# Branch C's projection beside the last head of branch A, its result kept in DRAM

## The chip, the cores and the metric

The kernel runs on one core of one Trainium2 chip. The metric is the device time of one execution in microseconds, from runs of the kernel before on the chip: 1801.05, 1803.37 and 1803.6, median 1803.37. Lower is better.

Five engines run their own instruction streams and wait for each other by semaphores: TensorE (PE in the profile, its weight loads PEld), VectorE (DVE), ScalarE (ACT), GpSimd (POOL) and SyncE (SP), which here only issues DMAs. POOL, too, issues DMAs.

## The reference, cut to what matters

The function is a small encoder trunk over one sequence of 512 positions, model width 1024, two layers, float32:

```
for l in range(DEPTH):
    xn = rms_norm(x, ln1[l])
    z = xn @ w_in[l]
    a_q, a_i, a_ff, a_fb, a_g, b_u, b_v, c_q, c_k, c_v, gz = jnp.split(z, offsets, axis=-1)
    o_a = hgrn2_bidirectional(a_q, a_i, a_ff, a_fb, lower[l])
    y_a = rms_norm(o_a, a_norm[l]) * silu(a_g)
    y_b = spatial_gating(gelu(b_u), gelu(b_v), w_s[l], b_s[l])
    y_c = window_attention(qh, kh, vh, sink[l])
    gates = sigmoid(gz)
    merged = gates[0] * (y_a @ w_br[l, 0]) + gates[1] * (y_b @ w_br[l, 1]) + gates[2] * (y_c @ w_br[l, 2])
    x = x + merged @ w_out[l]
    hn = rms_norm(x, ln2[l])
    x = x + square(relu(hn @ w_up[l])) @ w_down[l]
return rms_norm(x, final_norm)
```

Branch A is a gated linear recurrence in both directions with four heads, branch B a gated mixing of blocks of positions, branch C a windowed attention. What the change touches is the three products with w_br, their gates and their sum, and the order of the first loads and last stores.

## The kernel before, in words

**Products.** Each float32 product is made of three matmuls of a rounded part and a remainder (high by high, high by low, low by high), lines L193 to L195, L233 to L235 and, for the form of seven products out of eight, L396 to L398. A weight chunk of 128x1024 (512 KB) is loaded by SP into one of two buffers wr, cast by ACT to its high part wh (L188), and DVE subtracts that for the low part wl (L189); wh and wl have two buffers each. Chunks of the seven-product form (wq) are loaded into ten buffers of their own. An accumulator is 128x512 in PSUM; there are four kinds (m, a, c, s) of two.

**Stages.** A layer has a stage for the input projections, where the gates of branches A and C (tanh values, thd) are written to DRAM; a stage of the branches; a stage in which the branch outputs are projected, gated, added and multiplied by w_out (y, mT, wo); and the two feed-forward products (up, dA to dC). Memory in SBUF is given out by stage: buffers of one stage lie where those of the last one lay, and their first writer waits for the last users of that memory.

**The stage of the branches.** `a_head` (L517) computes a head of branch A: seven blocks of scores (at), each out of two exponentials on ACT and products and sums on DVE; then twice a transpose (kT), its copy, a state (stp, st); then the sum av, its norm by way of POOL (rs, L253), the scaled ao, its transpose oT and the head's output on. Each step waits for the one before on another engine. `c_scores` and `c_out` are branch C. `merge_b` (L827) is one of eight parts of B: a gate projection (gz, 24 matmuls), a product yB (12 matmuls), and the gated product mg, which POOL stores to DRAM (mgd, L837). `gate_a` (L841) projects A's output gate (ag, 24 matmuls), four times.

**What sets the order.** A scheduler of the framework puts the instructions of a stage in a fixed order per engine when the program is built. It takes those of the smallest number first that can run; `hp()` puts a statement ahead of the others, and `later(n)` adds n to the number, so that merge_b and gate_a (30000) fill the places where a head or branch C (15000) waits. They are emitted by `fill(0)` behind head 1, `fill(1, 2)` behind head 2, and `fill(3, 4, 5, 6, 7)` behind head 3.

**The stage after.** `gated` (L980) takes A's output and then C's: four gates th are loaded by POOL (L986), 48 matmuls y of `proj_tok` fill four accumulators, DVE multiplies by the gates (L994 for A, L996 for C) and adds C's to A's (L997); this twice for the two halves of the columns (fl). In C's turn PE transposes the sums (mT, L1002), DVE adds B's part (mB, loaded from mgd, L1005), and ACT and DVE split the result into the operands mgh and mgl of wo.

**The start and the end.** The first loads stand in one block with `hp()` (L632 to L653), the first weight chunk in two halves (L642). At the end `done` (L1061) sums squares of the finished rows, and `finish` (L1048) scales rows 0 and 1 or 2 and 3 of the four row tiles and stores them, all stores from SP (L1059).

## Time and profile before

| | us |
|---|---|
| runs | 1801.05, 1803.37, 1803.6 |
| profiled execution, its own time | 1803.97 |
| its span, first to last instruction | 1802.2 |
| PE busy in the span | 1713.4 |
| DVE busy | 1300.1 |
| ACT busy | 1014.7 |
| POOL busy | 128.6 |

The mean granted clock of TensorE over the span is 0.986 of full speed. A row of the timeline gives the start and length in microseconds, the engine, the line, the operation, output and inputs by their names in the program, the tile's size and the number of instructions in the row; in brackets stands how long the engine had been idle, and what it then waited for. A row of the waits gives the total, the number and the longest of the waits of one line for another. A row of the windows gives for a stretch of time the busy time of PE, PEld, DVE, ACT and POOL with their instructions, then the granted clock as a share of full speed, the DMA share and GB/s. The ends of PE's rows are modelled, its starts are measured.

### The profile page before, as it was taken

What the parts mean: (1) busy time and instruction counts of PE and PEld (TensorE: products, weight loads), DVE (VectorE), ACT (ScalarE), POOL (GpSimd) and SP (SyncE); (2) the same over time, 40 slices, a digit from 0 to 9 for tenths busy, and PEclk for the clock granted to TensorE, in tenths of its full rate; (3) what the DMA queues carried; (4) which work ended last, traced back from release to release, by engine and by line L of the source; (5) the groups of instructions that cost most, each with busy time, mean ns of one, the idle gap of its engine ahead of it and who ended that gap; (6) DMA issues with size and microseconds to landing.
All of it is one profiled execution on the core that took longest, in us unless ns stands there. A gap on an engine that the chain in (4) does not pass through costs nothing.

```text
span 1802.2 us, 21912 instructions
## 1 busy us (share of the span) xinstructions
PE 1713.4 (95%) x8024; PEld 1411.0 (78%) x8024; DVE 1300.1 (72%) x2005; ACT 1014.7 (56%) x1704; POOL 128.6 (7%) x177
## 2 busy tenths in 40 slices
PE   5999998999899999999999999899988999999997
PEld 4778877888687888888877887787877878888786
DVE  6886987677465757677889769767674666586867
ACT  5555578666324645454665565878862345545454
POOL 1011210000210000000010112000003000000000
PEclk9999999999899999999999999999999999999999
DMA  7232221222444242332332422121225352332321
GB/s 287 94 134 84 86 71 43 81 83 76 163 153 175 71 139 81 119 100 99 129 117 79 144 91 73 65 71 65 66 75 202 125 187 95 105 105 94 99 77 47
DMA packets 55994, 191.44 MB, mean 106 GB/s; under 512 B 7376, under 2 KB 7888, under 8 KB 55888
## 3 DMA queue, kind: packets, MB, share of 16 engines
q1 hardware_dynamic: 45648, 156.49, 25.9%
q0 software_dynamic: 10240, 33.56, 5.1%
q8 instruction: 63, 1.03, 0.2%
q14 instruction: 43, 0.35, 0.1%
HBM read 173.25 MB, written 16.78 MB: 105 GB/s over the span
## 4 chain that ended last, share of the span: by engine, by line
PE 51%; DVE 6%; ACT 5%; issue 5%; DMA 1%; SPq 0%; POOL 0%; DVEq 0%; POOLq 0%; ACTq 0%
PE up L195 6%; PE up L193 6%; PE up L194 6%; PE dA L396 3%; PE dA L397 3%; PE dA L398 3%; PE dC L396 2%; PE dC L397 2%; PE dC L398 2%; DVE wl L189 2%; ACT wh L188 1%; PE y L233 1%; PE at L524 1%; PE y L234 1%; PE y L235 1%
## 5 line engine op out<-in xcount | busy, mean ns | idle before, releaser
L189 DVE TENSOR_TENSOR wl<-wr,wh 128x1024 fp32r<-128x1024 f32 x171 | 209.6, 1225 | 182.5 <-ACT wh L188 181.8
L188 ACT CAST wh<-wr 128x1024 fp32r<-128x1024 f32 x171 | 179.3, 1049 | 264.5 <-PE up L194 97.7
L188 ACT CAST wh<-wq 128x1024 fp32r<-128x1024 f32 x196 | 206.2, 1052 | 216.4 <-PE dA L397 48.7
L189 DVE TENSOR_TENSOR wl<-wq,wh 128x1024 fp32r<-128x1024 f32 x196 | 238.9, 1221 | 106.9 <-ACT wh L188 102.9
L193 PE MATMUL up<-xh,wh 128*128 128x512 f32 x512 | 199.4, 391 | 3.8 <-ACT wh L188 1.9
L194 PE MATMUL up<-xl,wh 128*128 128x512 f32 x512 | 200.0, 391 | 0.3 <-DVE xl L245 0.2
L195 PE MATMUL up<-xh,wl 128*128 128x512 f32 x512 | 199.1, 390 | 0.8 <-DVE wl L189 0.7
L193 PEld LDWEIGHTS up<-xh,wh 128*128 128x128 f32 x512 | 96.1, 188 | 26.7 <-ACT wh L188 4.5
L195 PEld LDWEIGHTS up<-xh,wl 128*128 128x128 f32 x512 | 96.1, 188 | 22.1 <-DVE wl L189 2.5
L194 PEld LDWEIGHTS up<-xl,wh 128*128 128x128 f32 x512 | 96.1, 188 | 21.2 <-DVE xl L245 1.8
L396 PE MATMUL dA<-wh,sh 128*128 128x512 f32 x256 | 100.8, 394 | 0.5
L397 PE MATMUL dA<-wh,sh 128*128 128x512 f32 x256 | 99.8, 390 | 0.0
L398 PE MATMUL dA<-wl,sh 128*128 128x512 f32 x256 | 89.6, 391 | 0.0
L566 DVE TENSOR_TENSOR ex<-ex 128x512 f32<-128x512 f32 x112 | 75.8, 694 | 4.0 <-ACT kt L541 3.4
L524 PEld LDWEIGHTS at<-qt,kt 128*128 128x128 f32 x448 | 57.7, 192 | 12.5 <-ACT kt L541 6.6
L524 PE MATMUL at<-qt,kt 128*128 128x128 f32 x448 | 59.9, 277 | 6.8 <-DVE qt L539 5.9
L538 ACT ACTIVATE qt<-ex 128x512 f32<-128x512 f32 x56 | 37.7, 674 | 49.3 <-DVE ex L566 45.1
L253 POOL TENSOR_TENSOR rs<-ms,mhalf_t 128x4 f32<-128x4 f32 (+1 forms) x14 | 18.0, 1287 | 606.1 <-DVE ms L251 585.2
L396 PEld LDWEIGHTS dA<-wh,sh 128*128 128x128 f32 x256 | 48.0, 188 | 14.2 <-ACT wh L188 4.3
L398 PEld LDWEIGHTS dA<-wl,sh 128*128 128x128 f32 x256 | 47.9, 188 | 10.3 <-DVE wl L189 0.2
L397 PEld LDWEIGHTS dA<-wh,sh 128*128 128x128 f32 x256 | 48.1, 188 | 9.8
L193 PE MATMUL gz<-xh,wh 128*128 128x512 f32 x128 | 51.4, 401 | 3.9 <-ACT wh L188 3.8
(387 smaller groups left out, 4396.3 us busy)
## 6 DMA issues: line engine op xcount, KB each, us to landing
wr<-in_ws_dram SPq DMA_DIRECT2D x171, 512.0 KB, 3.3
wq<-in_ws_dram SPq DMA_DIRECT2D x112, 512.0 KB, 4.1
thd<-zt POOLq DMA_DIRECT2D x32, 256.0 KB, 2.7
th<-thd POOLq DMA_DIRECT2D x32, 256.0 KB, 4.3
mgd<-mg POOLq DMA_DIRECT2D x16, 256.0 KB, 2.3
mB<-mgd POOLq DMA_DIRECT2D x16, 256.0 KB, 3.3
x<-in_xT_dram SPq DMA_DIRECT2D x8, 256.0 KB, 6.1
xt<-in_xt_dram SPq DMA_DIRECT2D x8, 256.0 KB, 5.2
```

The lines of the kernel that those rows point to most:

```text
L188: nc.scalar.copy(hi, raw)
L189: nc.vector.tensor_tensor(lo, raw, hi.bitcast(F32), ALU.subtract)
L193: nc.tensor.matmul(pt, whi, xhi, start=first, stop=False)
L194: nc.tensor.matmul(pt, whi, xlo, start=False, stop=False)
L195: nc.tensor.matmul(pt, wlo, xhi, start=False, stop=last)
L233: nc.tensor.matmul(pts[t], xh, hi[:, c], start=k == 0, stop=False)
L396: nc.tensor.matmul(pt, xh[:, t], hi[:, c], start=start and k == 0, stop=False, skip_group_check=True)
L397: nc.tensor.matmul(pt, xl[:, t], hi[:, c], start=False, stop=False, skip_group_check=True)
L398: nc.tensor.matmul(pt, xh[:, t], lo[:, c], start=False, stop=k == 3, skip_group_check=True)
L524: nc.tensor.matmul(pt[:, c], kk(st), qq[:, c], start=True, stop=True)
L538: nc.scalar.activation(qt.rearrange(shp, b=nb, h=2), e_q, AF.Exp)
L566: nc.vector.tensor_tensor(o_ap, o_ap, ap_of(ex, i_, [[istep, 2]] + z), ALU.add)
```

## The change

Four edits. First, C's projection (now yC) is emitted in the stage of the branches, under `later(30000)` behind the four `gate_a`. Its four gate tiles per half are loaded into buffers of that stage (tag ch, ten of them, which branch C's queries and keys also use), multiplied in place, and stored by POOL to a new DRAM tensor mcd: eight loads and eight stores of 256 KB more in this stage per layer, while the next stage loads mcd back (mC, eight loads) and has only A's projection (yA). The gates for C are read from DRAM as before. Second, `fill` is called with 0, 1, 2 behind head 1, with 3, 4 behind head 2, and with 5, 6, 7 behind head 3. Third, the first loads and splits stand in blocks with `hp()` of their own. Fourth, the last scalings: rows 0 and 1 of the second half stay one operation of DVE; all others are multiplied by the final norm's weights on DVE earlier (in `done`) and then scaled on ACT; the stores leave from POOL (rows 2 and 3), SP and ACT.

```diff
@@ -630,27 +630,31 @@
 
     def x_load(k):
         t = T("l", "x")
-        nc.sync.dma_start(t, xT[:, k])
+        with hp():
+            nc.sync.dma_start(t, xT[:, k])
         x0.append(t)
 
+    x_load(0)
+
+    raw, hi, lo = sb.tile([P, CW], F32, tag="wr", bufs=WR, name=nm("wr")), *whl()
+    for i in range(2):
+        c = slice(i * S, (i + 1) * S)
+        with hp():
+            nc.sync.dma_start(raw[:, c], ws[CHUNK[(0, "bu", 0)], :, c])
+        with hp():
+            split(raw[:, c], hi[:, c], lo[:, c])
+    ready[(0, "bu", 0)] = hi, lo
+    x_load(1)
+    for i in (1, 2, 3):
+        x_load(2 * i)
+        x_load(2 * i + 1)
+        ready[(0, "bu", i)] = wload(0, "bu", i)
+    for i in range(8):
+        t = T("tv", "xt")
+        with hp():
+            nc.sync.dma_start(t, xt[:, i // 2, (i % 2) * S:(i % 2 + 1) * S])
+        x0r.append(t)
     with hp():
...
         id_t = const(ident, [P, P], name="id_t")
     n1 = norm_feat(0, x0, x0r)
     norm_rows(n1)
...
@@ -933,6 +938,15 @@
             for h, r in enumerate((lo64, hi64)):
                 nc.scalar.copy(yc[j][r, n * P:(n + 1) * P], po[r, h * P:(h + 1) * P])
 
+        def gates(tag, i, fl):
+
+            res = []
+            for t in range(4):
+                z = T(tag, "th")
+                nc.gpsimd.dma_start(z, thd[:, i * 4 + t, fl * S:(fl + 1) * S])
+                res.append(z)
+            return res
+
         def fill(*ds):
             with later(30000):
                 for d in ds:
@@ -959,59 +973,56 @@
         c_run(1)
         c_run(2)
         c_run(3)
-        fill(0)
+        fill(0,1,2)
         with later(15000):
             c_out(*prev)
         head(2)
-        fill(1, 2)
+        fill(3,4)
         head(3)
-        fill(3, 4, 5, 6, 7)
+        fill(5,6,7)
         with later(30000):
             for h in range(4):
                 gate_a()
+
+            ys = y_split(yc, "yh")
+            for fl in range(2):
+                th = gates("ch", 0, fl)
+                pts = proj_tok(ys, "yC", (l, "y", 2, fl), 0)
+                for t in range(4):
+                    with hp():
+                        nc.vector.scalar_tensor_tensor(th[t], th[t], 1.0, pts[t], ALU.add, ALU.mult)
+                    nc.gpsimd.dma_start(mcd[:, fl * 4 + t], th[t])
         end("br")
         begin("Y2")
-        mg = [[None, None] for _ in range(4)]
         ms = [None] * KT
-        grp = 0
-
-        def gated(bi, br, ys):
-            nonlocal grp
-            for fl in range(2):
-                th = []
-                for t in range(4):
-                    z = T("th", "th")
-                    nc.gpsimd.dma_start(z, thd[:, (1 - bi) * 4 + t, fl * S:(fl + 1) * S])
-                    th.append(z)
-                pts = proj_tok(ys, f"y{br}", (l, "y", br, fl), grp)
-                grp ^= 1
-                for t in range(4):
-                    with hp():
-                        if bi == 0:
-                            mg[t][fl] = T("mg", "mg")
-                            nc.vector.scalar_tensor_tensor(mg[t][fl], th[t], 1.0, pts[t], ALU.add, ALU.mult)
-                        else:
-                            nc.vector.scalar_tensor_tensor(th[t], th[t], 1.0, pts[t], ALU.add, ALU.mult)
-                            nc.vector.tensor_tensor(mg[t][fl], mg[t][fl], th[t], ALU.add)
...
         for h in range(4):
             nc.vector.scalar_tensor_tensor(oa[h], oa[h], 0.5, sg[h], ALU.mult, ALU.mult)
-        gated(0, 0, y_split(oa, "yi"))
-        gated(1, 2, y_split(yc, "yh"))
+        ys = y_split(oa, "yi")
+        for fl in range(2):
+            th = gates("th", 1, fl)
+            mc = []
+            for t in range(4):
+                m = T("mg", "mC")
+                nc.gpsimd.dma_start(m, mcd[:, fl * 4 + t])
+                mc.append(m)
+            pts = proj_tok(ys, "yA", (l, "y", 0, fl), 1 - fl)
+            for t in range(4):
+                with hp():
+                    nc.vector.scalar_tensor_tensor(th[t], th[t], 1.0, pts[t], ALU.add, ALU.mult)
+                    nc.vector.tensor_tensor(mc[t], mc[t], th[t], ALU.add)
+            for d in range(4 * fl, 4 * fl + 4):
+                pt = PT("c" if fl else "s", "mT")
+                for t in range(4):
+                    nc.tensor.transpose(pt[:, t * P:(t + 1) * P], mc[t][:, (d % 4) * P:(d % 4 + 1) * P], id_t)
+                hi, lo = T("yi", "mgh", F32R), T("yi", "mgl", F32R)
+                m = T("th", "mB")
+                nc.gpsimd.dma_start(m, mgd[:, d])
+                with hp():
+                    nc.vector.tensor_tensor(m, m, pt, ALU.add)
+                    split(m, hi, lo)
+                ms[d] = (hi, lo)
         xr = [[T("l", "xr"), T("l", "xr")] for _ in range(4)]
@@ -1020,8 +1031,7 @@
                 nc.gpsimd.dma_start(xr[t][fl], xsrc[:, t, fl * S:(fl + 1) * S])
         n2 = norm_tok("ln2", l, xr, False)
         for fl in range(2):
-            pts = proj_tok(ms, "wo", (l, "wo", fl), grp)
-            grp ^= 1
+            pts = proj_tok(ms, "wo", (l, "wo", fl), 1 - fl)
             for t in range(4):
                 with hp():
                     nc.vector.scalar_tensor_tensor(xr[t][fl], pts[t], 0.5, xr[t][fl], ALU.mult, ALU.add)
@@ -1052,11 +1062,12 @@
             rc = rstd_c(ss, D)
             for fl in range(2):
                 for i, t in enumerate(ts):
-                    if fl == 0 and ts[0] == 0:
+                    if (t // 2, fl) == (0, 1):
+                        nc.vector.scalar_tensor_tensor(xr[t][fl], xr[t][fl], rc[:, i:i + 1], fn_t[fl], ALU.mult, ALU.mult)
+                    else:
                         nc.scalar.activation(xr[t][fl], xr[t][fl], AF.Copy, scale=rc[:, i:i + 1])
-                    else:
-                        nc.vector.scalar_tensor_tensor(xr[t][fl], xr[t][fl], rc[:, i:i + 1], fn_t[fl], ALU.mult, ALU.mult)
-                    nc.sync.dma_start(out[:, t, fl * S:(fl + 1) * S], xr[t][fl])
+                    q = nc.gpsimd if t > 1 else nc.sync if fl else nc.scalar
+                    q.dma_start(out[:, t, fl * S:(fl + 1) * S], xr[t][fl])
 
         def done(t, fl):
 
@@ -1067,10 +1078,11 @@
                 ts = (t - 1, t)
                 if not last:
                     n1.turn(fl, ts)
-                elif t == 1 and fl == 0:
+                    return
+                if (t, fl) != (1, 1):
                     for i in ts:
-                        nc.vector.tensor_tensor(xr[i][0], xr[i][0], fn_t[0], ALU.mult)
-                elif (t, fl) in ((3, 0), (1, 1)):
+                        nc.vector.tensor_tensor(xr[i][fl], xr[i][fl], fn_t[fl], ALU.mult)
+                if (t, fl) in ((3, 0), (1, 1)):
                     finish(ts)
 
         for qd in range(4):
```

How the order moves, at three places. The first is PE at the end of the last head in layer 0 (av and oT are of that head, y and yA the first product of the next stage). Before:

```order
L609 MATMUL av_3568<-st_3542,qd_3546 128x128
L609 MATMUL av_3568<-st_3561,qd_3565 128x128
L609 MATMUL av_3568<-vt_539,at_3421 128x128
L609 MATMUL av_3568<-st_3542,qd_3546 128x128
L621 MATMUL oT_3591<-id_t,ao_3589 128x128 x4
L233 MATMUL y_886_4036<-wh_4042,yh_4012 128x512
```

and with the change, at oT and at the end of yC:

```order
L235 MATMUL yC_4111<-wl_4146,yh_4013 128x512
L233 MATMUL yC_4112<-wh_4145,yh_4013 128x512
L234 MATMUL yC_4112<-wh_4145,yl_4014 128x512
L621 MATMUL oT_3698<-id_t,ao_3696 128x128 x4
L235 MATMUL yC_4112<-wl_4146,yh_4013 128x512
L233 MATMUL yC_4109<-wh_4145,yh_4017 128x512
L234 MATMUL yC_4109<-wh_4145,yl_4018 128x512
```

```order
L233 MATMUL yC_4112<-wh_4145,yh_4017 128x512
L234 MATMUL yC_4112<-wh_4145,yl_4018 128x512
L235 MATMUL yC_4112<-wl_4146,yh_4017 128x512
L233 MATMUL yA_4221<-wh_4227,yh_4189 128x512
L233 MATMUL yA_4222<-wh_4227,yh_4189 128x512
```

Behind av stood oT and then y at once; now 35 matmuls of yC stand ahead of oT and 13 behind it, and 12 and 16 more further ahead (not shown). On ACT and POOL at the same place, with the semaphores that each row waits for (DMASW are those of POOL's own DMAs; on is a head's output, yh its high part), the changed program has

```order
L188 CAST wh_4227<-wr_4225 128x1024 [waits DMAHW1_49,DVE_49,PE_49]
L623 ACTIVATE on_3703<-oT_3698,vec_t 128x512 [waits PE_49]
L188 CAST wh_4257<-wr_4255 128x1024 [waits DMAHW2_49,DVE_49,PE_49]
L241 CAST yh_4189<-on_1559 128x512 [waits DMASW3_49,DMASW4_49,DMASW2_49,DMASW5_49,DMASW1_49,DMASW6_49,DMASW0_49,DMASW7_49,DVE_49,Activation_49]
L241 CAST yh_4193<-on_2367 128x512
```

```order
L994 DMA mcd<-th_4105 128x512 [waits DMASW6_49,DVE_49]
L994 DMA mcd<-th_4107 128x512 [waits DMASW7_49,DVE_49]
L946 DMA th_4205<-thd 128x512 [waits DMASW4_49,DMASW5_49,DMASW0_49,DMASW6_49,PE_49,DMASW7_49,Activation_49,Pool_49]
L946 DMA th_4207<-thd 128x512 [waits DMASW1_49]
L946 DMA th_4209<-thd 128x512 [waits DMASW2_49]
```

The eight semaphores of POOL's queues in the row of yh include the last four stores of mcd, since its buffer lies where the tiles th of those stores lie; before, the same row waited for the stores of mgd. The loads of the gates for yA (thd) stand behind the stores too.

The second place is PE on the way from the projections to the next layer. The transposes mT of the fifth block of columns (the operand mgh of wo, 4417 before and 4434 now, is made of it) ended like this before,

```order
L1002 MATMUL mT_4412<-id_t,mg_4184 128x128
L1002 MATMUL mT_4424<-id_t,mg_4184 128x128
L1002 MATMUL mT_4412<-id_t,mg_4186 128x128
L1002 MATMUL mT_4424<-id_t,mg_4186 128x128
L234 MATMUL wo_4477<-wh_4513,mgl_4314 128x512
L235 MATMUL wo_4477<-wl_4514,mgh_4313 128x512
L234 MATMUL wo_4478<-wh_4513,mgl_4314 128x512
```

with 20 wo matmuls in all (three of them shown) and eight transposes of the next blocks before the first wo that reads mgh_4417. Now:

```order
L1018 MATMUL mT_4429<-id_t,mC_4355 128x128
L1018 MATMUL mT_4441<-id_t,mC_4355 128x128
L1018 MATMUL mT_4453<-id_t,mC_4349 128x128
L1018 MATMUL mT_4453<-id_t,mC_4351 128x128
L1018 MATMUL mT_4453<-id_t,mC_4353 128x128
L1018 MATMUL mT_4453<-id_t,mC_4355 128x128
L1018 MATMUL mT_4465<-id_t,mC_4349 128x128
L1018 MATMUL mT_4465<-id_t,mC_4351 128x128
L1018 MATMUL mT_4465<-id_t,mC_4353 128x128
L1018 MATMUL mT_4465<-id_t,mC_4355 128x128
L233 MATMUL wo_4494<-wh_4560,mgh_4434 128x512
```

The last transpose of the block (mT_4429) stands nine transposes ahead of its reader. Further on, at the turn to layer 1, the broadcast bc of the norm (rs, made by POOL) among the matmuls of bu, before and now:

```order
L193 MATMUL bu_7661<-xh_7226,wh_7695 128x512
L194 MATMUL bu_7661<-xl_7227,wh_7695 128x512
L193 MATMUL bu_7662<-xh_7226,wh_7695 128x512
L260 MATMUL bc_7536<-id_t,rs_7526 128x128 x4
L195 MATMUL bu_7659<-xh_7226,wl_7696 128x512
```

```order
L193 MATMUL bu_7678<-xh_7225,wh_7682 128x512
L194 MATMUL bu_7678<-xl_7226,wh_7682 128x512
L193 MATMUL bu_7679<-xh_7225,wh_7682 128x512
L194 MATMUL bu_7679<-xl_7226,wh_7682 128x512
L260 MATMUL bc_7553<-id_t,rs_7543 128x128 x4
L195 MATMUL bu_7676<-xh_7225,wl_7683 128x512
L195 MATMUL bu_7677<-xh_7225,wl_7683 128x512
```

It stood behind 31 matmuls of bu, and stands behind eight.

The third place is SP's queue at the start (wr_87 is the first weight chunk in halves, wr_102 the second, wq the eight chunks of the seven-product stage, x the transposed input, xt the input by rows). Before, behind vec_t, one wq, the first x and seven wq:

```order
L178 DMA wq_397<-in_ws_dram 128x1024
L642 DMA wr_87<-in_ws_dram 128x512
L168 DMA wr_102<-in_ws_dram 128x1024
L642 DMA wr_87<-in_ws_dram 128x512
L633 DMA x_96<-in_xT_dram 128x512
L633 DMA x_98<-in_xT_dram 128x512
```

and now:

```order
L137 DMA vec_t<-in_vec_dram 128x58
L643 DMA wr_87<-in_ws_dram 128x512
L178 DMA wq_384<-in_ws_dram 128x1024
L137 DMA id_t<-in_ident_dram 128x128
L168 DMA wr_102<-in_ws_dram 128x1024
L178 DMA wq_386<-in_ws_dram 128x1024
L178 DMA wq_388<-in_ws_dram 128x1024
L634 DMA x_85<-in_xT_dram 128x512
L178 DMA wq_390<-in_ws_dram 128x1024
L634 DMA x_96<-in_xT_dram 128x512
```

```order
L168 DMA wr_112<-in_ws_dram 128x1024
L634 DMA x_118<-in_xT_dram 128x512
L634 DMA x_120<-in_xT_dram 128x512
L655 DMA xt_128<-in_xt_dram 128x512
L643 DMA wr_87<-in_ws_dram 128x512
L655 DMA xt_130<-in_xt_dram 128x512
```

The first half of wr_87 stands first and the first x eighth; the second half stands 23rd, behind all of wq and x.

More of the change, by code (lines that the diff above doesn't have):

```diff
@@ L632, in x_load @@
         t = T("l", "x")
-        nc.sync.dma_start(t, xT[:, k])
+        with hp():
+            nc.sync.dma_start(t, xT[:, k])
         x0.append(t)
-    with hp():
-        x_load(0)
-        raw, hi, lo = sb.tile([P, CW], F32, tag="wr", bufs=WR, name=nm("wr")), *whl()
-        for i in range(2):
-            c = slice(i * S, (i + 1) * S)
-            nc.sync.dma_start(raw[:, c], ws[CHUNK[(0, "bu", 0)], :, c])
-            split(raw[:, c], hi[:, c], lo[:, c])
-        ready[(0, "bu", 0)] = hi, lo
-        x_load(1)
-        for i in (1, 2, 3):
-            x_load(2 * i)
-            x_load(2 * i + 1)
-            ready[(0, "bu", i)] = wload(0, "bu", i)
-        for i in range(8):
-            t = T("tv", "xt")
-            nc.sync.dma_start(t, xt[:, i // 2, (i % 2) * S:(i % 2 + 1) * S])
-            x0r.append(t)
+    x_load(0)
[17 more added lines that the diff above has]
+        x0r.append(t)
+    with hp():
         id_t = const(ident, [P, P], name="id_t")
@@ L661, in trunk @@
     mgd = dram.tile([P, KT, S], F32, name="mgd")
+    mcd = dram.tile([P, 8, S], F32, name="mcd")
     for l in range(DEPTH):
@@ L977, in trunk @@
         ms = [None] * KT
-        grp = 0
-        def gated(bi, br, ys):
-            nonlocal grp
-            for fl in range(2):
-                th = []
-                for t in range(4):
-                    z = T("th", "th")
-                    nc.gpsimd.dma_start(z, thd[:, (1 - bi) * 4 + t, fl * S:(fl + 1) * S])
-                    th.append(z)
-                pts = proj_tok(ys, f"y{br}", (l, "y", br, fl), grp)
-                grp ^= 1
-                for t in range(4):
-                    with hp():
-                        if bi == 0:
-                            mg[t][fl] = T("mg", "mg")
-                            nc.vector.scalar_tensor_tensor(mg[t][fl], th[t], 1.0, pts[t], ALU.add, ALU.mult)
-                        else:
-                            nc.vector.scalar_tensor_tensor(th[t], th[t], 1.0, pts[t], ALU.add, ALU.mult)
-                            nc.vector.tensor_tensor(mg[t][fl], mg[t][fl], th[t], ALU.add)
-                if bi == 1:
-                    for d in range(4 * fl, 4 * fl + 4):
-                        pt = PT("s" if grp == 0 else "c", "mT")
-                        for t in range(4):
-                            nc.tensor.transpose(pt[:, t * P:(t + 1) * P], mg[t][fl][:, (d % 4) * P:(d % 4 + 1) * P], id_t)
-                        hi, lo = T("yi", "mgh", F32R), T("yi", "mgl", F32R)
-                        m = T("th", "mB")
-                        nc.gpsimd.dma_start(m, mgd[:, d])
-                        with hp():
-                            nc.vector.tensor_tensor(m, m, pt, ALU.add)
-                            split(m, hi, lo)
-                        ms[d] = (hi, lo)
```

## The prediction

> **What bounds the kernel now.** I read the page's table of busy time first.
>
> ```profile
> PE 1713.4 (95%) x8024; PEld 1411.0 (78%) x8024; DVE 1300.1 (72%) x2005; ACT 1014.7 (56%) x1704; POOL 128.6 (7%) x177
> ```
>
> TensorE (PE) works 1713.4 of 1802.2 us, so it is the bound, and an edit that leaves its work alone can win at most the 89 us in which it stands still, and what its clock loses around them. The change leaves the matmuls as they are (7122 rows of PE against 7123). So the second view was PE's waits over the whole span, by what ended them.
>
> ```profile
> PE bu L193 <- ACT wh L241: 17.0, 1, 17.0
> PE oT L621 <- DVE ao L617: 6.6, 2, 3.3
> ```
>
> The columns are total, times and longest. Apart from the start (17.0) the longest come twice, once per layer: oT, the end of a head's chain. The third view was PE's timeline around it, layer 0, from the last head's end to the first matmuls of the next stage (y); the bracket holds the idle time before a row and its releaser.
>
> ```profile
> 455.80 1.65 PE L586 MATMUL stp<-vt,kT 128*128 128x128 f32 x6 [2.73 <-ACT kT L583]
> 458.65 1.65 PE L586 MATMUL stp<-vt,kT 128*128 128x128 f32 x6 [0.57 <-ACT kT L583]
> 461.45 0.80 PE L609 MATMUL av<-st,qd 128*128 128x128 f32 x2 [0.72 <-DVE st L593]
> 468.95 0.85 PE L621 MATMUL oT<-id_t,ao 128*128 128x128 f32 x4 [3.29 <-DVE ao L617]
> 471.15 2.07 PE L233 MATMUL y<-wh,yh 128*128 128x512 f32 x4 [1.36 <-ACT yh L241]
> 473.02 0.63 PE L234 MATMUL y<-wh,yl 128*128 128x512 f32 x1
> 473.45 0.63 PE L235 MATMUL y<-wl,yh 128*128 128x512 f32 x1
> 477.24 0.39 PE L234 MATMUL y<-wh,yl 128*128 128x512 f32 x1
> ...
> 479.98 0.39 PE L234 MATMUL y<-wh,yl 128*128 128x512 f32 x1
> ```
>
> No wide matmul stands between those steps: the head's chain is bare. Idle: 2.73 + 0.57 + 0.72 + 3.29 + 1.36 = 8.67 us. And the clock falls: a 128x512 matmul follows the last after 0.43 us at 473 (473.45 - 473.02) and after 0.228 from 477.24 to 479.98, which is twelve steps. The windows view gives its size (PE, PEld, DVE, ACT, POOL busy, then the granted clock):
>
> ```profile
> 450.00:475.00 25.00, 16.34 (x67) 13.39 (x67) 11.41 (x21) 11.00 (x30) 5.69 (x10) 0.68 0.19 58
> 1325.00:1350.00 25.00, 20.57 (x112) 16.92 (x110) 18.20 (x30) 14.79 (x34) 0.00 (x0) 0.93 0.19 64
> 1350.00:1375.00 25.00, 20.13 (x81) 16.76 (x82) 9.38 (x14) 6.00 (x15) 10.24 (x19) 0.80 0.56 198
> ```
>
> Layer 0: 25 x (1 - 0.68) / 0.5 = 16 us at half clock, of which 2.65 idle; half of the other 13.4 is lost: 6.7, and about 0.5 more before 476. In all 8.7 + 7.2 = **16 us**. Layer 1's waits in 1338 to 1366:
>
> ```profile
> PE oT L621 <- DVE ao L617: 3.3, 1, 3.3
> PE stp L586 <- ACT kT L583: 2.8, 2, 2.2
> PE y L233 <- ACT yh L241: 1.3, 1, 1.3
> PE at L524 <- ACT kt L541: 0.9, 1, 0.9
> PE av L609 <- DVE st L593: 0.7, 1, 0.7
> PE kT L581 <- ACT kd L578: 0.4, 1, 0.4
> ```
>
> 9.4 idle, and 25 x (0.07 + 0.20) / 0.5 = 13.5 at half clock, 2.6 of it idle, half of 10.9 lost: 5.4. **14.8 us**. These two seams, 31 us, are what the change works on.
>
> **The change part by part.**
>
> C's projection as filler. Its 96 matmuls per layer (21.9 us at 0.228) now stand between the steps of the last head. Layer 0 has 35 of them (8.0 us) where PE waited 3.29 for ao, 12 before av's second half and 16 before the first stp. What is left there is about 1.2 us (stp after stp). Layer 1 has none between its last two at blocks and too few before the first stp: 3.7 left, by the waits above for at (1.3, since one more at is bare), kT and stp (2.0).
>
> The new wait. The tiles that C's gated product is stored from give their memory to the next stage. ScalarE's first split of A's output (yh), without which no yA matmul starts, therefore waits until the last four stores to DRAM have landed; behind it on ScalarE stand the other three splits and the weight casts, and on POOL the eight loads for yA. Nothing fills PE then. The chain from the last yC matmul, out of rows for the like before:
>
> ```profile
> 482.67 2.73 DVE L994 SCALAR_TENSOR_TENSOR mg<-th,y 128x512 f32<-128x512 f32 x4 [1.31 <-PE y L235]
> 483.65 2.58 POOL L986 DMA_DIRECT2D th<-thd  x4 [2.58 <-DVE mg L994]
> DMA to landing us min/median/max: 2.2/2.3/4.5
> 470.48 2.18 ACT L241 CAST yh<-on 128x512 fp32r<-128x512 f32 x4
> ```
>
> 0.68 for the product (2.73 / 4), 0.29 until POOL issues (483.65 less 482.67 + 0.69), 2.3 for a landing (the third row is of tile mg, whose stores are the same 256 KB), 0.62 for the cast (the first y matmul, at 471.15, starts 0.67 after it), and 0.2 between: 4.1 us, or 6.3 with the slowest landing. The gaps of 3.29 were followed by half clock, so I add one stretch of 3.4 us at half pace: 1.7.
>
> Left over: layer 0 1.2 + 4.1 + 1.7 = 7.0, layer 1 3.7 + 4.1 + 1.7 = 9.5. Gain 9.0 + 5.3 = **14.3** (10 to 19: the slow landing twice and a second slow stretch below, no slow stretch above). The eight loads for yA issue at 0.54 each, and are wanted only after yA's 48 first matmuls (10.9 us), so they hide; without that cover a landing would cost its 2.3 us or more.
>
> B's merge spread over the heads. The same 16 half-steps fill heads 1 to 3, only earlier. A bare at step costs what one costs now:
>
> ```profile
> 286.41 1.13 PE L524 MATMUL at<-qt,kt 128*128 128x128 f32 x8 [2.28 <-DVE qt L539]
> ```
>
> By the order it has no more at steps without filler than before. I take -1.5 (-10 to +8, four bare steps fewer or more).
>
> Transposes before wo. Behind yA the transposes for the fifth block now stand right before the wo matmuls that read it, with only 9 transposes between; before, 20 wo matmuls lay between as well. What is late is the chain add, cast:
>
> ```profile
> 518.11 1.03 PE L1002 MATMUL mT<-id_t,mg 128*128 128x128 f32 x8
> 521.08 1.27 DVE L1007 TENSOR_TENSOR mB<-mB,mT 128x512 f32<-128x512 f32 x2
> 521.79 1.22 ACT L241 CAST mgh<-mB 128x512 fp32r<-128x512 f32 x2 [2.62 <-DVE mB L1007]
> ```
>
> 0.64 + 0.07 + 0.61 + 0.1 = 1.4, less 9 transposes at 0.1 (8 take 1.03 with the last one's run-out): 0.5 per layer, **+1.0** (0 to 3, nothing of it covered).
>
> The turn to layer 1. The broadcast of the norm (bc, one block of transposes on PE) stands after 8 matmuls of bu instead of 31, and needs POOL's power:
>
> ```profile
> 916.89 0.39 PE L193 MATMUL bu<-xh,wh 128*128 128x512 f32 x1
> 917.46 0.67 DVE L242 TENSOR_TENSOR xs<-sf,xs 128x512 fp32r<-128x512 f32 x1
> 917.62 4.16 POOL L253 TENSOR_TENSOR rs<-ms,mhalf_t 128x4 f32<-128x4 f32 x1 [1.06 <-DVE ms L251]
> ...
> 920.47 0.41 DVE L358 TENSOR_TENSOR sf<-xf 128x256 f32<-128x256 f32 x1
> ...
> 923.92 1.05 PE L260 MATMUL bc<-id_t,rs 128*128 128x128 f32 x8
> 1165.97 1.04 POOL L253 TENSOR_TENSOR rs<-ms,mhalf_t 128x4 f32<-128x4 f32 x1 [9.98 <-DVE ms L251]
> ```
>
> Before, rs was ready at 921.78, two us ahead of bc. Now PE is at bc 1.8 us after bu starts (918.7 on this scale). DVE's input to it (ms) stands one weight split earlier, at about 0.4 us; rs then ends at 921.4 if the power takes 4.16 again (wait 2.7), at 918.3 if it takes the 1.04 of the head's (no wait). The nearer row is the one of this place, and a wait of that length may cost clock, like the 2.73 and 3.29 at the seam. I take **+3.0** (0 to 5.5). The Trainium skill ("SBUF — State Buffer", SBUF: two separate sides) says that VectorE's operations with two SBUF inputs and a GpSimd operation that reads SBUF exclude each other for whole instructions. DVE runs without idle time from 917.46 to 920.88 in the rows above, and the power ends 0.9 behind it, so the trace agrees; by the rule the wait goes to 3.8, since DVE's row of such operations after ms is longer in the new order, and the term to 5.5 with the clock.
>
> The start. The order of need is only half reached: the first weight's second half stands 23rd in SP's queue, behind the other stage's eight chunks and all of x.
>
> ```profile
> 16.36 0.62 ACT L241 CAST wh<-wr 128x512 fp32r<-128x512 f32 x1 [6.84 <-DMA wr<-in_ws_dram]
> 17.62 1.04 ACT L188 CAST wh<-wr 128x1024 fp32r<-128x1024 f32 x1 [0.65 <-DMA wr<-in_ws_dram]
> 47.96 0.39 PE L396 MATMUL tA<-wh,xh 128*128 128x512 f32 x1
> ```
>
> Before, the first half landed at 16.3, a whole chunk of 0.5 MB 1.26 later, and the second half behind that, near 18.25, with 5.0 MB of loads in front of it. Now it has 7.5 MB in front: 2.5 x 2 x 1.26 = 6.3 later, 24.55. PE can begin near 12 (the first tile of x stands behind 2.25 MB, where the first half-weight stood behind 4.25: 2.0 x 2.52 = 5.0 before 16.3, and its cast), does 12 matmuls and waits. With the cast's 0.62 it goes on at 25.2; 84 matmuls (19.1), bc (0.65) and a slow stretch (1.7 to 2.5) end bu at 47.0, where the stage after it began at 48.0. I round to **-0.8** (-2 to +1).
>
> The end. Four of the last scalings move to ACT, ahead of the two squares on which the last sum hangs:
>
> ```profile
> 1790.32 2.74 DVE L1058 SCALAR_TENSOR_TENSOR xr<-xr,rs,fn 128x512 f32<-128x512 f32 x4 [0.81 <-POOL rs L253]
> 1793.82 0.63 ACT L292 ACTIVATE jk<-xr 128x512 f32<-128x512 f32 x1 [4.70 <-DVE xr L440]
> ```
>
> At 0.67 each (about what the square takes) from 1791.7 they end at 1794.4, so the squares start 0.6 later; the last stores leave on two queues instead of one, which gives a little back. **+0.5** (-0.5 to +1).
>
> Sum: -14.3 - 1.5 + 1.0 + 3.0 - 0.8 + 0.5 = -12.1. From the profiled execution's 1803.97 that is 1791.9; the median shown is 0.6 lower, so **1791 us**.
>
> **The rivals.**
>
> A. Full cover: the landing is quick, no clock falls behind it, rs comes in time, and the heads gain more than half of their bound. -14.3 - 3.4 (no slow stretch) - 6 (heads) + 1.0 - 0.8 + 0.5 = -23.0: 1780. For it: the filler is long enough in layer 0. Against: PE has nothing to do while the stores land.
>
> B. The wait takes the seam's place: landings of 4.5 and two slow stretches in each layer cost 2 x (2.2 + 1.7) = 7.8 more, and rs its 5.5: -6.5 - 1.5 + 1.0 + 5.5 - 0.8 + 0.5 = -1.8, 1802: no change that can be told. For it: the maximum of 4.5 was measured with the same bytes. Against: the median is 2.3.
>
> C. Slower: the merge that was the last head's filler is used up in heads 1 and 2, so their at steps stand bare later. Each bare step costs 2.3, or with a slow stretch behind every second one 3.1 on the mean. The sum without the heads' term is -10.6; 4 more such steps than now use the gain up, and 6 more give +8: 1811. For it: the quoted step of 2.28 is of this kind. Against: the new order shows filler before nearly all of them.
>
> D. The change does not do what it says at the start: PE gains nothing there since the second half lands late. That is in the sum, as -0.8 and not the 5 us that PE's earlier begin would promise; with those it would be 1787.
>
> **How the numbers follow.** The forecast with D 0.72 (1784 to 1799), A 0.12, B 0.10, C 0.06. The range for eight in ten: below to 1781, into A, since the seams may give 19; above to 1801, the unknown wait at its bound. A difference of over 0.2% (3.6 us) can be told here: 1799.8 and 1807. Faster: the forecast nearly whole (0.70), A, and a little of B (0.04): 0.86. Same: the rest of B, of the forecast, and some of C: 0.10. Slower: 0.04.
>
> **What would show it.** In the profile after: no wait over 1.5 us for ao, and yC matmuls where oT stood idle; a wait of 4 us of PE for yh, ended by ACT, which itself waited for stores to mcd; clock 0.5 for 3.4 us right behind it; about half a us before the wo matmuls of the fifth block; bc waiting for POOL near 2.7; PE beginning near 12 us, with a hole to 25. The forecast is wrong if PE's waits in the heads grow by over 10 us, or if yh waits over 8 us or not at all.

## The result, and the profile after

The changed kernel takes 1789.7 us (median of four runs, 1785.6 to 1791.6) against 1803.2 before: a ratio of 0.9924 [0.9904, 0.9945]. A second set of runs gave 1790.6 and 0.9926 [0.9913, 0.9939]. In that set one execution of the changed kernel (1921.84 us, granted clock 0.849) and one of the kernel before (2876.49 us, 0.557) ran slow and are not counted. The forecast of 1791 (1781 to 1801) holds. Its sum holds only because several terms that were off cancel, so the closeness of the total is in part luck.

Two executions of the changed kernel were profiled, 1785.58 us (span 1783.8) and 1793.55 (span 1791.8); the median lies between them. The parts of the span, by the starts of PE's first matmul of each stage:

| from, to | before | after, faster execution | after, slower one |
|---|---|---|---|
| start to the first tA | 47.96 | 49.30 | 50.10 |
| to the first f of the branches, layer 0 | 123.71 | 121.95 | 123.37 |
| branches and projections to the first wo, layer 0 | 347.23 | 332.54 | 334.17 |
| wo, both layers | 97.36 | 99.06 | 99.00 |
| up and down, layer 0 | 341.42 | 341.02 | 341.44 |
| turn to layer 1 and its projections | 147.65 | 149.89 | 154.27 |
| branches and projections, layer 1 | 350.27 | 343.25 | 342.65 |
| up and down, layer 1 | 336.45 | 336.38 | 336.33 |
| last matmul to the end | 10.12 | 10.44 | 10.44 |

The branches of the two layers give 14.7 + 7.0 us in the faster execution; start, wo, turn and end take some of it back. What PE waited for in the changed kernel, over the whole span, in the rows that bear on the change (total, times, longest):

```profile
PE bu L193 <- ACT xh L244: 11.4, 1, 11.4
PE yA L233 <- ACT yh L241: 10.8, 2, 5.5
PE bu L193 <- ACT wh L241: 10.6, 1, 10.6
PE bc L260 <- POOL rs L253: 2.6, 1, 2.6
PE wo L234 <- DVE mgl L242: 1.5, 2, 0.8
PE mT L1018 <- DVE mB L1023: 1.3, 2, 0.7
```

No oT is in the list any more. In its place stand three new waits: for yh (twice), for the second half of the first weight chunk, and for rs. The timeline at the first of them, layer 0:

```profile
472.62 2.33 POOL L994 DMA_DIRECT2D mcd<-th x4 [6.09 <-DVE th L993]
478.13 2.18 ACT L241 CAST yh<-on 128x512 fp32r<-128x512 f32 x4 [4.00 <-DMA mcd<-th]
478.80 2.07 PE L233 MATMUL yA<-wh,yh 128*128 128x512 f32 x4 [5.53 <-ACT yh L241]
```

ACT's cast waits for stores to mcd, as forecast. The last of the four was issued at 474.41 (472.62 + 2.33 - 0.54) and lets ACT go at 478.13, 3.7 us later, where the forecast had 2.3. The clock behind it and in layer 1 (PE, PEld, DVE, ACT, POOL busy, granted clock, DMA share, GB/s):

```profile
475.00:500.00 25.00, 21.20 (x91) 17.37 (x92) 11.80 (x17) 5.34 (x7) 12.81 (x24) 0.93 0.93 333
1350.00:1375.00 25.00, 19.68 (x81) 15.80 (x81) 11.27 (x16) 6.23 (x9) 14.21 (x27) 0.86 0.83 284
```

Right behind the waits it was 0.86 from 478 to 490 us and 0.76 from 1362 to 1370, which is 3.4 and 3.8 us at half clock.

### The profile page after: what moved, and what is told of

It is laid out like the page before. It is cut to its first block, busy times and chain, and to the rows that moved or that the text cites. A ratio compares the mean times of both kernels' runs of the same rounds, so it can differ in the third digit from the quotient of the medians.

```text
span 1783.8 us, 21956 instructions
## 1 busy us (share of the span) xinstructions
PE 1702.4 (95%) x8024; PEld 1401.7 (79%) x8024; DVE 1300.3 (73%) x2005; ACT 1016.8 (57%) x1708; POOL 150.2 (8%) x213
## 4 chain that ended last, share of the span: by engine, by line
PE 48%; issue 31%; DVE 11%; ACT 7%; POOL 2%; DMA 1%; SPq 0%; POOLq 0%; DVEq 0%; ACTq 0%
PE up L193 3%; PE up L195 3%; PE up L194 3%; DVE wl L189 3%; PE wo L234 2%; PE wo L235 2%; PE dA L396 2%; ACT wh L188 1%; PE wo L233 1%; PE dA L397 1%; PE dA L398 1%; PE gz L193 1%; PE gz L195 1%; PE gz L194 1%; PE po L937 1%
```

## The experiments

Each is compared with the kernel before; the changed kernel's own ratio, 0.9924 to 0.9926, is what it is to be read against.

**The changed kernel again.**

> The changed kernel once more, as the base for the three beside it: 1786 to 1792. The explanation so far (the store wait of 5.4 us per layer, a start that is 1.3 us later, heads of layer 0 that idle 6 us less) should show again in the same places; if the idle time of layer 0's heads comes back to 10, that term was chance.

1790.6 us, 0.9926 [0.9913, 0.9939]. Where the times come from is read from the slower of the two profiles above: yA waits 5.6 and 5.4 us there, the first tA starts at 50.10, and PE stands idle for 3.7 of the 150 us from 245 to 395, where the faster execution has 3.0 and the kernel before 8.5. All three are there again.

### Is the wait for yh a matter of memory?

```diff
-                th = gates("ch", 0, fl)
+                th = gates("z" if fl else "ch", 0, fl)
```

> C's gated product of the second half of the columns is made in four buffers that outlive the stage (tag z), so that the last four stores hold no memory that the next stage takes over. Theory A (PE's wait for yh is the landing of those stores): the wait of 5.5 and 5.3 us falls below 1.5, the half-clock stretch behind it (1.6) goes too, and the time falls by 10 to 14 us, to about 1778. Rival B (the loads of the gates and of C's part, which stand behind the stores on POOL, would be the next to be late): the wait comes back as a wait of the transposes mT or of wo, and the gain is 3 to 6: about 1785. If yh still waits 5 us, something else than the stores holds it, and the time stays.

1775.9 us, 0.9848 [0.9835, 0.9861]. With the last four products in other buffers the wait for yh is gone from PE's list. Branches and projections fall to 325.6 and 334.7 us, 7 and 8.5 less than in the changed kernel. Part comes back at wo, 3.4 us in each layer, where a wait stands that was not there:

```profile
PE mT L1018 <- DVE mC L1014: 5.0, 4, 2.3
PE mT L1018 <- DVE mB L1023: 1.3, 2, 0.7
```

So the memory that the stores still read is the cause of the new wait, and each layer pays 5.4 us of idle time plus the clock behind it. Not all of the gain is this: bc stands behind 31 matmuls again in this kernel, and the turn's stage, 147.7 us in place of 149.9, makes 2.2 of the 10.0 us between the two profiles.

### Merge order, and what stands among the stores

The next run keeps everything of the change but the merge's spread.

```diff
-        fill(0,1,2)
+        fill(0)
...
-        fill(3,4)
+        fill(1, 2)
...
-        fill(5,6,7)
+        fill(3, 4, 5, 6, 7)
```

> The change without the spreading of B's merge (parts 0, then 1 and 2, then 3 to 7, as before). Theory A (the spread took away the idle time of layer 0's heads): PE's waits in the heads of layer 0 rise from 4.6 to about 10 us again, and the time rises by 4 to 8, to about 1795. Rival B (those waits depend on where the scheduler happens to put a filler, and the spread is not what moved them): the time stays within 3 of the change, and the waits move to other places.

1803.9 us, 1.0005 [0.9995, 1.0015]. Neither theory had this: without the spread the whole gain is gone. In layer 0's heads only part of the idle time comes back (5.9 us from 245 to 395, against 3.0 with the spread and 8.5 before). The timeline of layer 0 behind them shows where the rest is:

```profile
476.96 0.60 POOL L994 DMA_DIRECT2D mcd<-th  x1 [0.60 <-DVE th L993]
478.16 0.54 POOL L994 DMA_DIRECT2D mcd<-th  x1 [0.60 <-DVE th L993]
478.69 2.14 POOL L1031 DMA_DIRECT2D xr<-in_xt_dram  x4
480.21 0.33 SPq L168 DMA_DIRECT2D wr<-in_ws_dram  x1
480.82 1.08 POOL L994 DMA_DIRECT2D mcd<-th  x2
488.86 2.18 ACT L241 CAST yh<-on 128x512 fp32r<-128x512 f32 x4 [9.44 <-DMA mcd<-th]
489.53 2.07 PE L233 MATMUL yA<-wh,yh 128*128 128x512 f32 x4 [11.11 <-ACT yh L241]
```

Four loads of the residual x for the next stage (xr, 256 KB each) now stand on POOL's queue between the second and the third store, and a weight chunk leaves SP. The last store is issued at 481.36 and lets ACT go at 488.86, 7.5 us later. In layer 1 the wait for yh is 12.44. Two causes are mixed: POOL's queue (the last two stores stand behind four issues), and the transfers that run beside them. The next run takes the queue away:

```diff
-                    nc.gpsimd.dma_start(mcd[:, fl * 4 + t], th[t])
+                    nc.scalar.dma_start(mcd[:, fl * 4 + t], th[t])
```

> The old merge order again (1803.9 in the run before), with the eight stores of C's gated product issued by ScalarE's queue instead of POOL's. In the run before, four loads xr of the next stage stood on POOL between the second and the third of the last four stores; these landed at 488.8 and PE waited 11.1 and 12.4 us for yh. Theory A (the last stores are late because of their place on POOL, and that is all that the merge order changes): the waits fall to 4 to 6 us, the time to 1790 to 1793. Rival B (the landing is slow because four loads and a weight chunk share the DMA engines, by whichever queue): the waits stay above 9, the time above 1799. Rival C (the old merge order costs in the heads): the waits fall, but the time stays above 1796.

1800.7 us, 0.9996 [0.9987, 1.0006].

```profile
476.12 2.21 POOL L1031 DMA_DIRECT2D xr<-in_xt_dram  x4
477.69 0.96 ACTq L994 DMA_DIRECT2D mcd<-th  x2
478.88 0.33 ACTq L994 DMA_DIRECT2D mcd<-th  x1
480.01 0.33 SPq L168 DMA_DIRECT2D wr<-in_ws_dram  x1
486.46 2.18 ACT L241 CAST yh<-on 128x512 fp32r<-128x512 f32 x4 [7.19 <-DMA wr<-in_ws_dram]
487.13 2.08 PE L233 MATMUL yA<-wh,yh 128*128 128x512 f32 x4 [8.91 <-ACT yh L241]
```

The last store leaves 2.5 us sooner, at 478.88, on another queue, and ACT still goes on only 7.6 us after it (the row names the weight chunk, but by the trace that landed 0.4 us after the cast had begun). yA waits 8.91 and 6.97 us, 2.2 and 5.5 less than with POOL's queue. None of the theories came as stated: the waits lie between those of A and B, and they fall while the time stays above 1796, as C has it. In the profile the turn's stage takes back 2.3 us of what the waits give (153.5 in place of 151.2). Last, the loads are taken out of the way, with the stores on POOL again: a column written from A's sums makes each load wait until branch A's first products are done.

```diff
...
                     nc.vector.tensor_tensor(mc[t], mc[t], th[t], ALU.add)
+            if fl == 0:
+                late = mc
...
+                nc.vector.tensor_copy(xr[t][fl][:, :1], late[t][:, :1])
                 nc.gpsimd.dma_start(xr[t][fl], xsrc[:, t, fl * S:(fl + 1) * S])
```

> The changed kernel with the merge's old order (as in the run of that name, 1803.9 us), and with the loads of the residual x for the next stage made to come after branch A's first products: one column of each x tile is first written from the sums of the first half, so that the load cannot start before them, and on POOL's queue all eight loads then stand behind the last stores and the loads of C's products. The computation is unchanged. If it was these loads among the last stores that made the wait of yA 11.1 and 12.4 us, the stores land within 2.3 to 4 us of their issue, yA waits 4.1 to 5.5 in both layers, and the time is 1790 to 1794. If the old merge order made the stores late by itself, the wait stays at 8 us or more in at least one layer, and the time at 1798 or above. The loads come later than before, and layers wait up to 2 us for them at wo's residual if that is too late.

1792.2 us, 0.9936 [0.9922, 0.9949], inside the first theory's range.

```profile
476.79 0.60 POOL L994 DMA_DIRECT2D mcd<-th  x1 [0.61 <-DVE th L993]
477.99 1.73 POOL L994 DMA_DIRECT2D mcd<-th  x3 [0.60 <-DVE th L993]
482.68 2.18 ACT L241 CAST yh<-on 128x512 fp32r<-128x512 f32 x4 [3.43 <-DMA mcd<-th]
483.35 2.08 PE L233 MATMUL yA<-wh,yh 128*128 128x512 f32 x4 [5.10 <-ACT yh L241]
1366.21 2.07 PE L233 MATMUL yA<-wh,yh 128*128 128x512 f32 x4 [4.76 <-ACT yh L241]
```

The four stores stand together again, the last, at 479.18, lets ACT go after 3.5 us, and the waits are 5.1 and 4.8 in place of 11.1 and 12.4. It was the loads among the stores, not the merge's order by itself: of the 6.0 and 7.7 us that they cost, 2.2 and 5.5 go with POOL's queue, and 3.8 and 2.2 only when the loads go too. That the latter is the transfers beside the stores is the likely reading; the run with ACT's queue also put the issues on ACT's list, and no run has the one without the other. In the changed kernel the four stores stand together. The Trainium skill ("DMA: Bandwidth & Descriptors", Queues, rings and completion order) has each DMA engine take turns between the queues that have work for it, a packet at a time, so that a queue of its own spares a store the transfers ahead of it but not those beside it. The 8.91 us with another queue, between 5.10 and 11.11, agree with that. One thing more fell out of this run: its transposes of the later blocks stand among the wo matmuls again, the waits of mT and wo are gone, and wo takes 47.45 us per layer in place of 49.5. That hides what the old order costs by itself: layer 0's branches and projections take 336.6 us here and 332.5 in the changed kernel.

The spread alone, on the kernel before:

```diff
-        fill(0)
+        fill(0,1,2)
...
-        fill(1, 2)
+        fill(3,4)
...
-        fill(3, 4, 5, 6, 7)
+        fill(5,6,7)
```

> The kernel before with B's merge spread (parts 0 to 2, 3 and 4, 5 to 7) and nothing else. Theory A (the spread itself is worth only the 2 us of idle time by which layer 0's heads differ between the two merge orders): 1800 to 1803, no difference that can be told, and PE's waits at the end of the last head as before (3.3 for ao, twice). Rival B (the spread is worth several us by itself): 1797 or less.

1799.1 us, 0.9977 [0.9967, 0.9987]: 3.6 us by the medians, between the two theories. The profiled execution is the fastest of its eight (1795.64), so its trace shows more than the median has. Its layer 0 gains 10 us by the trace (337.2 in place of 347.2), layer 1 nothing (351.8 in place of 350.3), and the turn loses 2.6, since bc now waits 2.96 for rs here too. The waits for oT stay at 3.3 each. Of the 10 us in layer 0, 5.9 are idle time of PE; the rest goes with a higher clock at the seam (0.86 in place of 0.78 from 445 to 470, 1.00 in place of 0.88 from 470 to 495).

### The start, and what it moves 900 us later

First the second half of the first weight chunk leaves on ACT's queue and no longer stands 23rd on SP's:

```diff
-            nc.sync.dma_start(raw[:, c], ws[CHUNK[(0, "bu", 0)], :, c])
+            (nc.scalar if i else nc.sync).dma_start(raw[:, c], ws[CHUNK[(0, "bu", 0)], :, c])
```

> The second half of the first weight chunk is issued by ScalarE's queue instead of SP's, where it stood 23rd. Theory A (that half alone makes the hole of 10.6 us at the start): the hole goes, bu ends 8 to 11 us earlier than 49.3, and the time falls by as much, to about 1781. Rival B (x, the sums for the seven-product stage and the weight casts come no earlier, so the hole only moves behind bu): the first tA starts at most 3 us earlier, about 1787.

1777.7 us, 0.9858 [0.9845, 0.9871]. PE's hole is gone and the first tA starts at 37.05 in place of 49.30. Of these 12.3 us 8.8 are given back in the stage behind (130.75 us in place of 121.95), where PE is idle for 7.7 us and not 3.8, among it in the wait below, which was not there. The granted clock of the stage is 0.96 and not 1.00; over 130.75 us that is 10 us at half clock, half of them lost, and makes the other 5.

```profile
PE tC L396 <- ACT gs L688: 2.8, 1, 2.8
```

A part of what the runs gain lies 900 us later. There the order has bc behind 31 matmuls of bu again, not 8, and PE does not wait for rs: the turn's stage takes 147.7 us. Then the whole block of first loads as before, with all else of the change:

```diff
-        with hp():
-            nc.sync.dma_start(t, xT[:, k])
+        nc.sync.dma_start(t, xT[:, k])
...
-    x_load(0)
+    with hp():
+        x_load(0)
...
```

> The change with the first loads of the kernel before. Theory A (the new start costs 1.3 us to the first tA, by the profile): 1787 to 1790, 1 to 2 below the change. Rival B (the start gains as it was meant to): 1791 or more. Rival C: the later stages take up any difference, 0.

1781.7 us, 0.9883 [0.9869, 0.9896], below what any of the theories had. The changed kernel is some 8 us faster without its new first loads. By the trace the stages up to the first f take 170.3 us, against 171.3 and 173.5 in the two executions of the changed kernel; bc is behind 31 matmuls and waits for nothing, and the turn's stage takes 147.5 against 149.9 and 154.3. These two stages make 3.3 of the 5.6 us to the faster execution and 9.9 of the 13.6 to the slower. The rest is in the branches, 0.4 to 2.0 in layer 0 and 1.5 to 2.1 in layer 1, and its cause was not isolated.

### Together

Other buffers and the half chunk by ACT in one kernel:

> The two edits together: the other buffers (14.7 us below the change) and the first weight's second half by ScalarE's queue (12.9 below). They work at different places, so if both gains are what their profiles show, they add: 1762 to 1765. Rival: part of either gain is a shift of clock stretches that the other takes away again: 1768 to 1774.

1770.8 us, 0.9822 [0.9808, 0.9835]. The start gives 5 us here and not the 12 of its own run: the kernel with the other buffers already had bc behind 31 matmuls, so that part is counted once. The time is in the rival's range, but what is counted twice is that order, not a stretch of lower clock.

Then C's second half is not sent through DRAM, since its four z tiles are free to keep it:

```diff
-                    nc.gpsimd.dma_start(mcd[:, fl * 4 + t], th[t])
+                    if fl == 0:
+                        nc.gpsimd.dma_start(mcd[:, fl * 4 + t], th[t])
+        kept = th
...
+                if fl:
+                    mc.append(kept[t])
+                    continue
```

> The kernel of the last run (the other buffers and the half chunk issued by ScalarE, 1770.8 us) with one thing more: the second half of branch C's gated product stays in the four z tiles that hold it, and is neither stored to DRAM nor loaded back; the first half still goes there and back. The computation is unchanged. If the new wait of the transposes for DVE's mC (2.33 in each layer since the stores hold no buffer of the next stage) is the landing of a load from DRAM that itself waits for a late store, it goes, and so does most of the 3.4 per layer that wo's segment gained: from wo to up 49.5 in place of 52.9, the time 1764 to 1767. If instead those transposes wait for DVE's own list of sums and products there, the wait stays near 2, the time at 1769 to 1772.

1763.9 us, 0.9782 [0.9768, 0.9797], the fastest kernel of the study: 39 us under the kernel before and 26 under the change. DVE's sums for these tiles are still made, and the transposes' wait for mC is gone; what is left around wo is the pair of short waits:

```profile
PE wo L234 <- DVE mgl L242: 1.5, 2, 0.8
PE mT L1023 <- DVE mB L1028: 1.3, 2, 0.7
```

wo takes 49.5 us per layer in place of 52.9, so that wait was the trip of C's second half through DRAM.

**The changed kernel's second profile.**

> The changed kernel once more, for its profile: the profiled execution of the first run was 1785.6 against a median of 1790. If the difference is the granted clock alone, this one shows the same waits (yA 5.3 to 5.5, bc 2.6, wo 0.8) and the extra time is spread over the stretches with the lower clock; if it is a wait that comes and goes, one of these waits is longer by 3 to 5 us.

1793.55 us. The truth lies between the two cases: yA waits as before (5.6 and 5.4 us), bc 4.2 in place of 2.6, and the clock falls behind bc in this execution. First the faster execution, then the slower:

```profile
902.15 4.59 POOL L253 TENSOR_TENSOR rs<-ms,mhalf_t 128x4 f32<-128x4 f32 x1
904.63 1.22 DVE L189 TENSOR_TENSOR wl<-wr,wh 128x1024 fp32r<-128x1024 f32 x1
906.80 1.16 PE L260 MATMUL bc<-id_t,rs 128*128 128x128 f32 x8 [2.63 <-POOL rs L253]
900.00:920.00 20.00, 17.37 (x83) 14.20 (x82) 15.83 (x32) 10.35 (x17) 5.72 (x3) 1.00 0.32 106
```

```profile
906.40 4.59 POOL L253 TENSOR_TENSOR rs<-ms,mhalf_t 128x4 f32<-128x4 f32 x1
911.04 2.07 PE L260 MATMUL bc<-id_t,rs 128*128 128x128 f32 x8 [4.16 <-POOL rs L253]
900.00:920.00 20.00, 15.84 (x64) 12.73 (x63) 13.53 (x28) 10.61 (x20) 6.26 (x4) 0.83 0.30 101
```

POOL's power takes 4.59 us in both. What differs is how early PE comes to bc, and the clock after it: 0.83 against 1.00 in these 20 us. PE is early by the clock ahead of it: from the first tA of layer 1 to the first bu it takes 7.8 us in the faster execution, with a granted clock of 0.78 there, and 6.2 in the slower one at full clock. These 1.5 us are the difference of the two waits, and bc starts 12.5 us behind that first tA in both. The turn's stage takes 4.4 us more, all of it behind bc. The remaining 3.6 us of the 8.0 between the spans are spread over other stages with a lower clock.

## Why the prediction was right, and which steps were not

**The forecast and the rivals.** A full cover (1780) and a wait that takes the whole gain back (1802) were each one edit away: the first is what other buffers give (1775.9), the second what xr loads among the stores give (1803.9), with one landing of 7.4 us or more in each layer where the rival had 4.5. The third rival, bare at steps, did not come; the opposite did.

**The seams.** The mechanism held, shown by taking the memory away. The terms of this step were mis-sized. The wait is 5.5 and 5.3 us, not 4.1: the term took one landing of 2.3 us, and the last of four stores in a row lands later (the four of layer 0 land 2.3 to 3.6 us after their issue; in the run with late loads, too, ACT goes on 3.5 us after its issue). A lower clock stands behind it in both layers, as forecast: 3.4 and 3.8 us at half clock, where 3.4 were taken. What is left of the old seam is less than forecast: 0.4 us (for the split before yC) in place of 1.2 in layer 0, and 1.6 (po waiting for pT 1.0, at 0.3, the split 0.3) in place of 3.7 in layer 1.

**The heads.** The step that failed is that spreading the merge leaves as many at steps without filler as before (-1.5). The order was read for the steps it leaves bare, not for the ones it newly covers. PE's busy time (the second number of a row) in most of the heads of layer 0, and in a window of it, before:

```profile
245.00:395.00 150.00, 141.48 (x769) 119.96 (x770) 108.33 (x262) 113.29 (x249) 8.16 (x10) 1.00 0.21 69
270.00:295.00 25.00, 20.47 (x117) 17.19 (x116) 18.53 (x51) 21.66 (x37) 2.03 (x2) 1.00 0.15 53
```

and after:

```profile
245.00:395.00 150.00, 146.97 (x804) 125.11 (x803) 110.77 (x267) 114.54 (x251) 11.95 (x17) 1.00 0.26 87
270.00:295.00 25.00, 23.98 (x136) 20.32 (x135) 19.57 (x54) 21.26 (x44) 1.84 (x2) 1.00 0.23 76
```

Idle time falls from 8.5 to 3.0 us; the bare step at 286 that the prediction quoted as its price is one of those filled. Layer 0's branches then add up: -9.0 for the seam as forecast, +1.4 for the longer wait, -0.8 for the smaller rest and -5.5 for the heads make -13.9, measured -14.7 and -13.1. In layer 1, -5.3 + 1.2 - 2.1 make -6.2 without any gain in the heads, measured -7.0 and -7.6. The run with the spread alone shows that the spread is enough for this: its idle time from 245 to 395 is 3.0 too, without any yC; layer 1 gains nothing there either (+1.5). But the changed kernel with the old order has 5.9, not 8.5, so with yC in the program some 2.6 of the 5.5 us come without the spread. What covers those places was not isolated.

**Before wo.** +0.5 per layer was forecast, with a bound of 1.5; 0.8 and 0.9 were measured: waits of 0.7 (transposes) and 0.8 (mgl) came, and a wait of 1.1 that stood there before went.

**The turn.** The wait was forecast at 2.7, the term at +3.0 (0 to 5.5). It is 2.63 and 4.16 us, the stage 2.2 and 6.6 longer, the latter beyond the term's bound. The row of the same place before (4.16 us for the power) was the right one to take, and 1.04 the wrong one. The 2.63 of the faster execution rests on the slow stretch ahead of bu. The profile before has it too (7.9 us from the first tA of layer 1 to bu), and the forecast took it over without naming it; the slower execution, which lacks it, has the 4.16. POOL's power took 4.15 to 4.68 us at this place in all kernels of the study. In the rows above DVE runs until 905.85 and the power ends 0.9 us behind it. The Trainium skill ("SBUF — State Buffer", SBUF: two separate sides) has VectorE's two-input operations and a GpSimd operation that reads SBUF shut each other out. The trace agrees with it. The wait of 3.8 and the term of 5.5 that the prediction worked out by it lie between those of the two executions; no run here took the lock away by itself.

**The start.** -0.8 was forecast (-2 to +1), and the two executions show +1.3 and +2.1, outside the range. In the faster one PE begins at 11.40 and stands still from 16.9 to 27.46, not to 25.2 (PE's rows, then ACT's ahead of the second):

```profile
11.40 2.07 PE L193 MATMUL bu<-xh,wh 128*128 128x512 f32 x4 [11.40 <-ACT xh L244]
27.46 0.79 PE L193 MATMUL bu<-xh,wh 128*128 128x512 f32 x1 [10.57 <-ACT wh L241]
24.45 0.60 ACT L241 CAST xs<-sf 128x512 fp32r<-128x512 f32 x1
24.96 0.72 ACT L244 ACTIVATE xh<-x,vec_t 128x512 fp32r<-128x512 f32 x1
25.58 0.61 ACT L276 ACTIVATE jk<-xt 128x512 f32<-128x512 f32 x1
26.20 0.71 ACT L278 ACTIVATE x<-x,vec_t 128x512 f32<-128x512 f32 x1
26.81 0.60 ACT L241 CAST wh<-wr 128x512 fp32r<-128x512 f32 x1
```

The landing came as forecast: the second half was issued at 18.17 and landed 6.4 us later, at 24.6, against 24.55. The step that failed is the one behind it. The forecast let the cast start at the landing, but ACT had begun xs and had xh, jk and x ahead of the cast in its order, and cast at 26.81 without having stood idle. That is the 2.3 us by which bu ends later than forecast (49.3 in place of 47.0). Rival D was right that the second half's place on the queue takes the gain. What the forecast did not see is the price of the edit as a whole, about 8 us by the run without it: it counted the turn as a result of the new order and did not connect it with the first loads. That connection is shown in one direction only. In the changed kernel each of three edits (other buffers, old start, half chunk by ACT) brought bc back behind 31 matmuls and removed the wait; but the spread alone also put it behind 8. Any edit can tip the scheduler there.

**The end.** +0.5 forecast, +0.3 measured (10.12 to 10.44), and 10.41 to 10.65 in every other kernel with the new end.

**The sum.** -12.1 was forecast. Without start, turn and end the faster execution has -22.2 where the forecast had -14.8; start, turn and end add 3.9 there and 9.1 in the slower one, where the forecast had 2.7. The total came out because the heads gained more than the forecast had, and the start and the turn lost more. In the faster execution another 1.8 came in the stage behind the start, for which the forecast had no term (0.3 in the slower one).

## What to carry to other kernels

A store to DRAM that closes a stage is not free because nobody reads it soon: its source buffer may be the next stage's first memory, and then the store's landing stands on the path. Keep the last stores' tiles out of the memory that the next stage writes first, or keep the tiles and drop the store. When a fixed order comes from a scheduler, look after every edit at which transfers it has put between the last stores, and at far places that the edit did not touch: two waits of 2 to 12 us moved here by edits elsewhere. When filler is moved, compare the waits it newly covers with the waits it uncovers, place by place.

## What the hardware showed that was not expected

Four stores of 256 KB in a row let their waiter go 3.5 us after the last issue with no other load than one weight chunk near them, and 7.5 us after with four loads of the same size among them; on another engine's queue it was still 7.6 after a somewhat earlier issue (all in layer 0). A power of 128x4 numbers on GpSimd took 4.59 us while VectorE ran without a gap, against 1.04 in the heads. Six profiled executions have PE's wait for rs at the turn. In the 10 us behind it the granted clock was 1.00 after waits of 2.32, 2.63 and 2.96 us, 0.83 after 2.97 and 4.17, and 0.70 after 4.16. So the length alone did not decide it near 3 us. What was different besides was the stretch ahead: PE was at 0.79 in the 8 us that end 5 us before bc in the four executions with the shorter waits, and at full clock in the two with the longer ones.
